# Gate and up projections by seven block products of 256 columns, the other engines' order from due times

## The chip, the cores and the metric

The kernel runs on one core of a Trainium2 chip. The metric is the time of one execution on the device in microseconds (us), the median of several runs. The core has a matmul engine (PE, with its weight loads shown apart as PEld) and three elementwise engines: DVE (VectorE), ACT (ScalarE) and POOL (GpSimd). SP is the queue that issues the weight transfers. PE writes to the accumulator memory PSUM, the other tiles lie in SBUF.

## The reference, cut to what matters

Two decoder layers on 512 tokens of width 1024 in float32. Each layer has a SwiGLU half step, a mixer and another SwiGLU half step: four half steps in all (`ffn` with j = 0 to 3). The change is to the half steps.

```python
D_MODEL, SEQ, D_FF = 1024, 512, 2816

def swiglu(x, wg, wu, wd):
    return (jax.nn.silu(x @ wg) * (x @ wu)) @ wd

h = x
for l in range(DEPTH):
    h = h + 0.5 * swiglu(rmsnorm(h, norm_ffn1[l]), ffn1_wg[l], ffn1_wu[l], ffn1_wd[l])
    hn = rmsnorm(h, norm_mix[l])
    ...
    h = h + mix.astype(h.dtype)
    h = h + 0.5 * swiglu(rmsnorm(h, norm_ffn2[l]), ffn2_wg[l], ffn2_wu[l], ffn2_wd[l])
return rmsnorm(h, final_norm)
```

## The kernel before

Activations are held transposed: 8 tiles `h[0]` to `h[7]` of 128 channels by 512 tokens. Every float32 operand of a matmul is split into a rounded part (hi) and the rest (lo), and `mm3` makes one product of blocks as three matmuls: hi by hi, lo by hi, hi by lo. Each matmul has 128x128 weights, loaded before it, and 512 moving columns, the tokens. In row names `pg<-xl,wh` the first input is the moving one, the second the weights.

A half step has 22 feature tiles of 128 features. For each, the gate tile `pg` and the up tile `pu` are made by `proj`: 8 channel blocks by `mm3`, 24 matmuls. DVE multiplies `pg` and `pu` by the row norm `rstd` (L316, L323), ACT takes Silu (L318), DVE multiplies the two (L325), ACT and DVE split the result into `ahi` and `alo` (L328, L329). The feature tiles come in parts of 8, 7 and 7; after each part eight down products `pd`, one per channel tile, add the part into `h[d]` (L372).

Weights are streamed once. `Stream` fetches units of 128x1024 floats (512 KB) into three raw buffers `wr`, ACT rounds each half into `wh` (L182), DVE subtracts to get `wl` (L186). In one stretch of the second mixer the subtraction is on POOL instead (L184).

At the start of a half step the sums of squares of `h` (`ssum`, L231 and L232) are turned into `rstd` by a short chain over PE, DVE, POOL, DVE, ACT, DVE, PE and ACT. For the very first half step DVE adds the squares between its first conversions; for the later ones POOL adds them at the end of the stage before.

The schedule is manual: every engine executes its instructions in the order in which the code issues them, and waits at the head of its own queue for semaphores. `W.pump()` after each tile decides where transfers and conversions are put: it converts two units ahead. No planner stands behind it.

## Time and profile before

| | us |
|---|---|
| median of 3 runs | 1925.91 (1925.67 to 1926.69) |
| the profiled execution, its own time | 1927.78 |
| its span, first to last instruction | 1926.0 |
| PE busy | 1906.6 |
| PEld busy | 1574.9 |
| DVE busy | 1015.7 |
| ACT busy | 723.0 |
| POOL busy | 206.4 |

The profiled execution is 1.87 us above the median, and 1.78 us of it lies outside the span. PE busy is a union of overlapping records: a 512-column matmul is recorded with 389 ns, while the next one starts sooner, so rates are read from starts and not from durations. Weight loads overlap the matmuls.

### The profile page before, as it was taken

How to read it: one execution, taken by the hardware profiler on the slowest of the kernel's cores; microseconds unless marked ns; L12 is line 12 of the kernel's file. 1: busy time of each engine (PE TensorE's matmuls, PEld its weight loads, DVE VectorE, ACT ScalarE, POOL GpSimd, SP SyncE). 2: the span in 40 equal slices, each digit the busy share in tenths (PEclk: the TensorE clock that was granted, in tenths of full speed). 3: DMA queues.
4: the chain of work that ended last, by engine and by line, in shares of the span. 5: the costliest groups of instructions: out<-in, count | busy, mean ns of one | idle time of the engine just before them, and what ended most of it. 6: DMA issues, size and time to landing. Idle time of an engine off the chain costs nothing.

```text
span 1926.0 us, 23329 instructions
## 1 busy us (share of the span) xinstructions
PE 1906.6 (99%) x8972; PEld 1574.9 (82%) x8972; DVE 1015.7 (53%) x1734; ACT 723.0 (38%) x1475; POOL 206.4 (11%) x267
## 2 busy tenths in 40 slices
PE   8999999999999999999999999999999999999998
PEld 6888888778888888888888888878887788888886
DVE  6534444656654344446444434566888654344443
ACT  5322222443432232224322323336888543222223
POOL 0000000203100000002000000113556410000001
PEclk9999999999999999999999999999999999999999
DMA  4323232221232222323322232242000233232322
GB/s 163 105 88 109 79 112 87 87 94 65 78 110 98 96 100 79 110 81 105 105 91 99 92 105 96 80 139 74 29 29 26 65 100 99 88 108 80 111 89 73
DMA packets 52751, 174.62 MB, mean 91 GB/s; under 512 B 6496, under 2 KB 8720, under 8 KB 52640
## 3 DMA queue, kind: packets, MB, share of 16 engines
q1 hardware_dynamic: 51328, 171.67, 26.9%
q8 instruction: 71, 1.16, 0.3%
q10 hardware_dynamic: 576, 1.05, 0.1%
q0 software_dynamic: 736, 0.41, 0.1%
q14 instruction: 40, 0.33, 0.1%
HBM read 171.01 MB, written 2.10 MB: 90 GB/s over the span
## 4 chain that ended last, share of the span: by engine, by line
PE 96%; DVE 1%; ACT 1%; DMA 1%; issue 1%; POOL 0%; SPq 0%; POOLq 0%; ACTq 0%
PE pg L292 8%; PE pg L291 8%; PE pu L291 8%; PE pg L293 8%; PE pu L293 8%; PE pu L292 8%; PE pd L292 8%; PE pd L293 8%; PE pd L291 8%; PE pj L291 3%; PE pj L293 2%; PE pj L292 2%; PE X L762 2%; PE S L997 2%; PE T L1044 2%; PE O L1078 1%
## 5 line engine op out<-in xcount | busy, mean ns | idle before, releaser
L186 DVE TENSOR_TENSOR wl<-wr,wh 128x512 fp32r<-128x512 f32 (+1 forms) x622 | 415.3, 710 | 150.0 <-ACT wh L182 150.0
L182 ACT ACTIVATE wh<-wr 128x512 fp32r<-128x512 f32 (+3 forms) x640 | 357.6, 605 | 262.7 <-PE pd L292 190.7
L291 PE MATMUL pg<-xh,wh 128*128 128x512 f32 x704 | 275.7, 392 | 5.8 <-ACT wh L182 5.2
L292 PE MATMUL pg<-xl,wh 128*128 128x512 f32 x704 | 275.4, 391 | 0.6 <-DVE xl L223 0.6
L293 PE MATMUL pg<-xh,wl 128*128 128x512 f32 x704 | 275.1, 391 | 0.0
L291 PE MATMUL pu<-xh,wh 128*128 128x512 f32 x704 | 274.3, 390 | 0.0
L293 PE MATMUL pu<-xh,wl 128*128 128x512 f32 x704 | 273.9, 389 | 0.0
L292 PE MATMUL pu<-xl,wh 128*128 128x512 f32 x704 | 273.9, 389 | 0.0
L291 PE MATMUL pd<-ahi,wh 128*128 128x512 f32 x704 | 273.9, 389 | 0.0
L292 PE MATMUL pd<-alo,wh 128*128 128x512 f32 x704 | 273.9, 389 | 0.0
L293 PE MATMUL pd<-ahi,wl 128*128 128x512 f32 x704 | 273.9, 389 | 0.0
L232 POOL TENSOR_TENSOR ssum<-ssum,sq 128x512 f32<-128x512 f32 x41 | 53.2, 1297 | 1456.3 <-issue 978.9
L328 ACT ACTIVATE ahi<-av 128x512 fp32r<-128x512 f32 x88 | 55.7, 633 | 377.4 <-DVE av L325 377.4
L372 DVE SCALAR_TENSOR_TENSOR h<-pd,h 128x512 f32<-128x512 f32 (+1 forms) x97 | 66.4, 686 | 228.3 <-PE pd L293 228.3
L291 PEld LDWEIGHTS pg<-xh,wh 128*128 128x128 f32 x704 | 132.9, 189 | 34.4 <-ACT wh L182 5.2
L292 PEld LDWEIGHTS pg<-xl,wh 128*128 128x128 f32 x704 | 132.9, 189 | 29.3 <-DVE xl L223 1.7
L323 DVE TENSOR_TENSOR t<-pu,rstd 128x512 f32<-128x512 f32 x88 | 60.8, 691 | 181.2 <-PE pu L293 181.2
L318 ACT ACTIVATE sg<-t 128x512 f32<-128x512 f32 x88 | 55.6, 632 | 266.8 <-DVE t L316 266.8
L293 PEld LDWEIGHTS pg<-xh,wl 128*128 128x128 f32 x704 | 132.8, 189 | 27.4
L291 PEld LDWEIGHTS pd<-ahi,wh 128*128 128x128 f32 x704 | 132.2, 188 | 27.5
L293 PEld LDWEIGHTS pu<-xh,wl 128*128 128x128 f32 x704 | 132.2, 188 | 27.5
L292 PEld LDWEIGHTS pd<-alo,wh 128*128 128x128 f32 x704 | 132.2, 188 | 27.4
(340 smaller groups left out, 2581.4 us busy)
## 6 DMA issues: line engine op xcount, KB each, us to landing
wr<-in_wts_dram SPq DMA_DIRECT2D x259, 512.0 KB, 3.5
wr<-in_wts_dram SPq DMA_DIRECT2D x64, 448.0 KB, 3.2
h<-in_xt_dram SPq DMA_DIRECT2D x8, 256.0 KB, 5.0
cb<-in_cbias_dram SPq DMA_DIRECT2D x8, 128.0 KB, 3.5
out_dram<-ot ACTq DMA_DIRECT2D x4, 256.0 KB, 4.5
wr<-in_wts_dram SPq DMA_DIRECT2D x2, 456.0 KB, 5.4
out_dram<-ot SPq DMA_DIRECT2D x3, 256.0 KB, 5.0
wr<-in_wts_dram SPq DMA_DIRECT2D x4, 128.0 KB, 4.8
```

The source lines that it names most:

```text
L182: S.activation(hi[:, c], self.raw[j][:, c], AF.Copy)
L186: V.tensor_sub(lo[:, c], self.raw[j][:, c], f32(hi[:, c]))
L232: eng.tensor_tensor(self.ssum, self.ssum, sq, op=OP.add)
L291: TE.matmul(out, wh, xh, start=first, stop=False)
L292: TE.matmul(out, wh, xl, start=False, stop=False)
L293: TE.matmul(out, wl, xh, start=False, stop=last)
L318: S.activation(sg, t1, AF.Silu)
L323: V.tensor_mul(t2, pu, nm.rstd)
L328: S.activation(ahi, av, AF.Copy)
L372: V.scalar_tensor_tensor(h[d][:, c], pd[:, c], 0.5, h[d][:, c], op0=OP.mult, op1=OP.add)
L762: TE.matmul(p, (hi, hi, lo)[i][:, c], (nm.xh, nm.xl, nm.xh)[i][k], start=n == 0, stop=n == 3 * KB - 1)
L997: TE.matmul(bk[:, c0:c0 + n], w[:, j * 128:(j + 1) * 128], keys[:, 0:n], start=start and j != 1, stop=stop, skip_group_check=True)
```

## The change

In each half step the first four feature tiles (two pairs, `PLAIN = 2`) are made as before. From the third pair on, the gate tiles of a pair (m even) and its up tiles (m odd) are made together, as a 2x2 block product in Winograd's form: the weights of two feature tiles are four blocks (two feature tiles by two channel halves of four blocks each), the activations four blocks (two channel halves by two token halves of 256), and seven products (numbered 1 to 7 in the code) take the place of eight. Each product is 4 blocks by `mm3` on 256 columns, 12 matmuls. There are 9 pairs, so 18 values of m, in each of the four half steps.

For this there are new operands. Sums of the activation blocks (`x_sums`, `x_dif`) are made once per half step, on DVE and ACT. Sums of the weight blocks (`T1` to `T4`) are made on POOL, four 128x512 operations per m. Five of the seven products use an operand that must then be split by ACT and DVE (`sh`, `sl`): T1 to T4 and the plain block B22. The other two use the blocks of the first raw unit, split as before. Partial results in PSUM are copied by ACT into `U` and combined by DVE between products, since later products accumulate on them.

The parts are 4, 4, 4, 4 and 6 tiles, and the down products of a part are put between the products of later m: `half_step` gives PE's order. From m = 5 to m = 20 one step of PE is 7 products and two down products of 12 matmuls (512 columns). A raw unit goes to one of three rings: `wr` (3 buffers), `wf` (1) and `wg` (2).

PE's order and SP's order of transfers are fixed by the code. The order on DVE, ACT and POOL is worked out at build: each step has a due time, counted back from PE's, and a list schedule with assumed costs picks the ready step that is due first; a POOL step and a DVE step marked `lock` are not put at the same time. The sorted order is then issued, so on the chip the order of every engine is fixed, as before. The order of the mixers is not changed.

```diff
 KB = D // 128
-PARTS = (8, 7, 7)
+PARTS = (4, 4, 4, 4, 6)
+PLAIN = 2
...
+def half_step():
...
+    ev = [(t, 2 * q + e) for q in range(PLAIN) for t in "gu" for e in range(2)]
+    m0, end = 2 * PLAIN, len(PARTS) - 1
+    d = [("d", p, i, 0, PARTS[p]) for p in range(end) for i in DORD]
+    for m in range(m0, 22):
+        x, y = (d.pop(0) if d and m > m0 else None for _ in range(2))
+        if m == m0:
+            ev += [(n, m) for n in (1, 2, 5, 6)]
+        else:
+            ev += [e for e in ((1, m), (2, m), (7, m - 1), (5, m), x, (6, m), (3, m - 1), (4, m - 1), y) if e]
+    ev += [(7, 21), (4, 21), (3, 21)] + [("d", end, i, 0, 4) for i in DORD[:2]]
+    return ev + [("d", end, i, 4 * (n < 2), PARTS[end]) for n, i in enumerate(DORD)]
+
...
+    class Step:
...
+        def add(self, eng, cost, fn, deps=(), bufs=(), lock=False):
...
+                for i in range(1, len(u)):
+                    f = u[i].touch[0]
+                    f.deps += [x for x in [u[i - 1].touch[0]] + (u[i - r.n].touch if i >= r.n else []) if x is not f]
...
+            at = 0
+            for s in steps:
+                if s.eng == "PE":
+                    s.due = at
+                    at += s.cost
...
+                if s.due is None:
+                    s.due = min([n.due - self.HOP for n in s.next] + [at]) - s.cost
...
+            free = {"PE": 0, "SP": 0, "DVE": 2000, "ACT": 1500, "POOL": 1500}
...
+                            continue
+                        other = held["POOL"] if e == "DVE" else held["DVE"] if e == "POOL" else 0
+                        begin = lambda s: max(free[e], ready[s], other if s.lock or e == "POOL" else 0)
+                        first_ = min(begin(s) for s in can[e])
+                        s = min((s for s in can[e] if max(free[e], ready[s]) <= first_ + 30), key=lambda s: (s.due, s.n))
+                        k = (begin(s), s.due)
...
+                (t, _), s, e = best
+                (can if e in can else line)[e].remove(s)
+                end = t + s.cost
+                free[e] = t + 1900 if e == "SP" else end
+                if s.lock or e == "POOL":
+                    held[e] = end
...
+            return [s for t, s in sorted(out, key=lambda x: (x[0], x[1].n))]
...
+        def run(self):
+            for s in self.order():
+                s.fn()
...
+            def x_sums(k):
+                g0, g1 = nm.gain(k), nm.gain(k + 4)
+                q, t, s = Buf(Rq), Buf(RU), Buf(Rx)
+                s1 = act(256, lambda: S.activation(q.t[:, A], h[k + 4][:, B], AF.Copy, scale=g1), (), (q,))
+                s1 = dve(325, lambda: V.scalar_tensor_tensor(t.t[:, A], h[k][:, B], g0, q.t[:, A], op0=OP.mult, op1=OP.add),
+                         (s1,), (q, t), True)
+                s2 = dve(325, lambda: V.scalar_tensor_tensor(t.t[:, B], h[k][:, A], g0, t.t[:, A], op0=OP.mult,
+                                                             op1=OP.subtract), (s1,), (t,), True)
+                s3 = dve(325, lambda: V.scalar_tensor_tensor(q.t[:, B], h[k + 4][:, A], g1, t.t[:, B], op0=OP.mult,
+                                                             op1=OP.add), (s2,), (q, t), True)
...
+                xsum[k] = (s, s2, s3)
+
+            def x_dif(k, dep):
...
+                s = dve(256, lambda: V.tensor_sub(q.t[:, A], h[k][:, A], h[k][:, B]), (), (q,), True)
+                s = act(256, lambda: S.activation(nm.xh[k][:, B], q.t[:, A], AF.Copy, scale=g), (s, dep), (q,))
+                xdif.append(dve(325, lambda: V.scalar_tensor_tensor(
+                    nm.xl[k][:, B], q.t[:, A], g, f32(nm.xh[k][:, B]), op0=OP.mult, op1=OP.subtract), (s,), (q,), True))
...
+                s1 = gps(sub(t["T1"], lambda: b1.t[:, H0], lambda: b0.t[:, H0]), (l0, l1), (t["T1"], b0, b1))
+                s2 = gps(sub(t["T2"], lambda: t["T1"].t, lambda: b1.t[:, H1]), (s1, l1), (t["T2"], t["T1"], b1))
+                s4 = gps(sub(t["T4"], lambda: b0.t[:, H1], lambda: t["T2"].t, OP.add), (s2, l0), (t["T4"], t["T2"], b0))
+                s3 = gps(sub(t["T3"], lambda: b1.t[:, H1], lambda: b1.t[:, H0]), (l1,), (t["T3"], b1))
...
+            def operand(n, m):
+
...
+                w = Buf(Rs)
+                s = act(T, lambda: S.activation(w.t[0], src(), AF.Copy), (dep,), (w, b))
+                return w, dve(T, lambda: V.tensor_sub(w.t[1], src(), f32(w.t[0])), (s,), (w, b), True)
...
+            def product(n, m):
+                u = m % 2
+                if n == 1:
+                    u0, u1 = load("wf" if u else "wr"), load("wg")
+                    convert(u0)
+                    pair[m] = {"w": con[u0], "r1": raw[u1], "t": sums(m, raw[u0], raw[u1]), "xy": Buf(Rxy)}
...
+                dep += {5: [x[1] for x in xsum.values()], 3: [x[2] for x in xsum.values()], 7: xdif}.get(n, [])
+                dep += [p[x] for x in {6: ("e2", "e2c"), 7: ("e6",), 4: ("e7",), 3: ("e7c",)}.get(n, ())]
+                acc = z if n in (5, 3) else xy
...
+                def mm():
+                    o, q, r = {1: (0, A, 0), 2: (4, A, 0), 7: (0, B, 0), 4: (4, B, 0), 5: (0, slice(0, 256), 1),
+                               6: (0, slice(256, 512), 1), 3: (0, slice(512, 768), 1)}[n]
+                    out, (hi, lo) = acc.t[:, B if n == 2 else A], ws()
...
+                        start = k == 0 and n in (1, 5)
+                        TE.matmul(out, wh, xh[:, q], start=start, stop=False, skip_group_check=True)
+                        TE.matmul(out, wh, xl[:, q], start=False, stop=False, skip_group_check=True)
+                        TE.matmul(out, wl, xh[:, q], start=False, stop=k == 3, skip_group_check=True)
+
+                done = p[n] = pe(1440, mm, dep, (w, acc))
...
+                if n == 2:
+                    U = p["U"] = Buf(RU)
+                    p["c"] = c0, c1 = [Buf(Rcu if u else Rcg) for _ in range(2)]
+                    p["e2"] = act(256, lambda: S.activation(U.t[:, B], xy.t[:, A], AF.Copy), (done,), (xy, U))
+                    p["e2c"] = dve(256, lambda: V.tensor_add(c0.t[:, A], xy.t[:, B], U.t[:, B]), (p["e2"],), (xy, U, c0))
+                    return
+                if n in (1, 5):
...
+                if n == 6:
+                    p["e6"] = act(256, lambda: S.activation(U.t[:, A], xy.t[:, A], AF.Copy), (done,), (xy, U))
+                elif n == 7:
+                    p["e7"] = act(256, lambda: S.activation(U.t[:, B], xy.t[:, A], AF.Copy), (done, p["e2c"]), (xy, U))
+                    p["e7c"] = dve(256, lambda: V.tensor_add(c1.t[:, B], z.t[:, A], U.t[:, B]), (p["e7"], p[5]), (z, U, c1))
+                elif n == 3:
+                    p["e3"] = dve(256, lambda: V.tensor_add(c1.t[:, A], z.t[:, A], U.t[:, A]), (done, p["e6"]), (z, U, c1))
+                if 3 in p and 4 in p:
+                    x1 = dve(256, lambda: V.tensor_mul(c0.t[:, A], c0.t[:, A], nm.rstd[:, A]), (p["e2c"], rstd), (c0,), True)
+                    y = dve(T, lambda: V.tensor_mul(c1.t, c1.t, nm.rstd), (p["e3"], p["e7c"], rstd), (c1,), True)
+                    x2 = dve(256, lambda: V.tensor_mul(c0.t[:, B], xy.t[:, A], nm.rstd[:, B]), (p[4], rstd), (xy, c0))
+                    if not u:
+                        sg[m] = [(c0, act(T, lambda: S.activation(c0.t, c0.t, AF.Silu), (x1, x2), (c0,))),
+                                 (c1, act(T, lambda: S.activation(c1.t, c1.t, AF.Silu), (y,), (c1,)))]
...
+                        s = sg.pop(m - 1)
+                        finish(m // 2, 0, c0, (x1, x2), s[0])
+                        finish(m // 2, 1, c1, (y,), s[1])
...
+            def down(p, d, k0, k1):
+                f0, n = sum(PARTS[:p]), PARTS[p]
+                if k0 == 0:
+                    u = load("wr")
+                    convert(u)
+                    pds[d] = (Buf(Rpd), con[u])
...
+                s = pe(681 * (k1 - k0), mm, [*ends] + [ah[f0 + k][1] for k in range(k0, k1)],
+                       [w, b] + [ah[f0 + k][0] for k in range(k0, k1)])
```

Two places in the program's order on DVE, of before and of the change.

The first is DVE at the start of the first half step, from the conversion of the second weight unit on (`wl`), with the sums of squares (`ssum`). Before:

```order
L186 TENSOR_TENSOR wl<-wr,wh 128x512 x2
L232 TENSOR_TENSOR ssum<-ssum,sq 128x512 x3
L186 TENSOR_TENSOR wl<-wr,wh 128x512 x4
L232 TENSOR_TENSOR ssum<-ssum,sq 128x512 x4
L266 TENSOR_SCALAR var<-pn 128x4
L277 TENSOR_SCALAR sq<-ident,rc 128x128 x4
L279 TENSOR_TENSOR dgl<-sq,dgh 128x512
```

After the change the same place on DVE reads as follows; `U`, `xs` and `sq` of 128x256 are the block sums of `x_sums`:

```order
L218 TENSOR_TENSOR wl<-wr,wh 128x512 x2
L271 TENSOR_TENSOR ssum<-ssum,sq 128x512 x3
L796 TENSOR_TENSOR ssum<-ssum,sq 128x512 x4
L628 SCALAR_TENSOR_TENSOR U<-h_72,vec,sq 128x256
L630 SCALAR_TENSOR_TENSOR U<-h_72,vec,U 128x256
L632 SCALAR_TENSOR_TENSOR sq<-h_76,vec,U 128x256
L628 SCALAR_TENSOR_TENSOR U<-h_73,vec,sq 128x256
L630 SCALAR_TENSOR_TENSOR U<-h_73,vec,U 128x256
L637 TENSOR_TENSOR xs<-sq,xs 128x256
L632 SCALAR_TENSOR_TENSOR sq<-h_77,vec,U 128x256
L636 TENSOR_TENSOR xs<-U,xs 128x512 x2
L541 TENSOR_TENSOR wl<-wr,wh 128x512 x6
```

The conversion of the third and fourth unit (`wl` x4 before, the first of `wl` x6 now) stood after three sums of squares; it now stands behind all seven and behind the block sums of two channel blocks. ACT's order has the same shift: its conversion of the third unit stands behind its squares and the copies for those block sums.

The second place is DVE inside the first half step, between matmul tiles, with buffer numbers in the names. Before, for one feature tile and the start of the next:

```order
L329 TENSOR_TENSOR alo_373<-av_370,ahi_372 128x512
L186 TENSOR_TENSOR wl_402<-wr_249,wh_401 128x512 x2
L316 TENSOR_TENSOR t1_409<-pg_376,rstd_336 128x512
L186 TENSOR_TENSOR wl_439<-wr_312,wh_438 128x512 x2
L323 TENSOR_TENSOR t2_446<-pu_413,rstd_336 128x512
L325 TENSOR_TENSOR av_448<-sg_411,t2_446 128x512
L329 TENSOR_TENSOR alo_451<-av_448,ahi_450 128x512
```

After the change, from the first combination of an m (L721) on, in the steady stretch; `sl` are the split operands of T1 to T4, `cg` and `cu` the combined gate and up tiles:

```order
L721 TENSOR_TENSOR cg_1648<-xy_1593,U_1643 128x256
L541 TENSOR_TENSOR wl_1646<-wf_1548,wh_1645 128x512 x2
L730 TENSOR_TENSOR cu_1673<-z_1469,U_1457 128x256
L677 TENSOR_TENSOR sl_1670<-T4_1403,sh_1669 128x512
L677 TENSOR_TENSOR sl_1691<-T3_1589,sh_1690 128x512
L769 SCALAR_TENSOR_TENSOR h1_73<-pd_1677,h1_73 128x512
L541 TENSOR_TENSOR wl_1713<-wr_1611,wh_1712 128x512
L677 TENSOR_TENSOR sl_1732<-T1_1641,sh_1731 128x512
L732 TENSOR_TENSOR cu_1673<-z_1469,U_1457 128x256
L677 TENSOR_TENSOR sl_1748<-T2_1675,sh_1747 128x512
L736 TENSOR_TENSOR cu_1465<-xy_1407,rstd_400 128x256
L606 TENSOR_TENSOR cu_1465<-cu_1465,cg_1279 128x512
```

For the work of one m DVE had eight 128x512 operations. It now has ten of 128x512 and five of 128x256, on average over gate and up, and among them stand the conversion (`wl`) and the addition into `h` of two down products, one 128x512 operation each.

## Rows read from the trace of the kernel before

**Rows 1.** The page: busy us (share of the span) per engine, granted clock in 40 slices.

```profile
PE 1906.6 (99%) x8972; PEld 1574.9 (82%) x8972; DVE 1015.7 (53%) x1734; ACT 723.0 (38%) x1475; POOL 206.4 (11%) x267
...
PEclk9999999999999999999999999999999999999999
```

**Rows 2.** The page: the chain that ended last, shares by engine.

```profile
PE 96%; DVE 1%; ACT 1%; DMA 1%; issue 1%; POOL 0%; SPq 0%; POOLq 0%; ACTq 0%
```

**Rows 3.** Windows: third half step: length, busy us of PE, PEld, DVE, ACT, POOL.

```profile
902.00:1262.00 360.00, 360.00 (x1593) 298.22 (x1592) 172.70 (x263) 110.95 (x199) 11.95 (x13) 1.00 0.29 97
```

**Rows 4.** Timeline, PE at 400 us (start, us): 512 columns, twelve matmuls apart.

```profile
400.22 0.39 PE L293 MATMUL po<-wh,xl 128*128 128x512 f32 x1
...
402.94 0.39 PE L293 MATMUL po<-wh,xl 128*128 128x512 f32 x1
```

**Rows 5.** Timeline, PE at 1305 us: 304 columns, 58 matmuls apart.

```profile
1305.53 0.30 PE L292 MATMUL pj<-wl,xh 128*128 128x304 f32 x1
...
1313.62 0.30 PE L293 MATMUL pj<-wh,xl 128*128 128x304 f32 x1
```

**Rows 6.** Timeline, PE at 1318 us: two matmuls of 256 columns and the next.

```profile
1318.61 0.40 PE L997 MATMUL S<-kA,qA 128*128 128x256 f32 x2
1318.85 0.28 PE L1005 MATMUL S<-negb,identb 128*128 128x256 bf16 x1
```

**Rows 7.** Groups by line and form: busy us, mean ns: the loads of those 256-column matmuls.

```profile
L997 PEld LDWEIGHTS S<-kA,qA 128*128 128x128 f32 x128 | 23.1, 190 | 2.7 <-ACT P L1023 0.9
```

**Rows 8.** Groups by line and form, DVE, ACT and POOL: busy us, mean ns.

```profile
L186 DVE TENSOR_TENSOR wl<-wr,wh 128x512 fp32r<-128x512 f32 x551 | 382.5, 732 | 150.0 <-ACT wh L182 150.0
L182 ACT ACTIVATE wh<-wr 128x512 fp32r<-128x512 f32 x569 | 328.5, 619 | 262.7 <-PE pd L292 190.7 <-issue 46.8 <-DMA wr<-in_wts_dram 15.2
...
L316 DVE TENSOR_TENSOR t<-pg,rstd 128x512 f32<-128x512 f32 x88 | 60.8, 691 | 122.1 <-PE pg L293 119.8 <-ACT rstd L287 2.2
...
L232 POOL TENSOR_TENSOR ssum<-ssum,sq 128x512 f32<-128x512 f32 x41 | 53.2, 1297 | 1456.3 <-issue 978.9 <-ACT sq L231 477.5
...
L223 DVE SCALAR_TENSOR_TENSOR xl<-h,vec,xh 128x512 fp32r<-128x512 f32 x48 | 37.9, 798 | 37.3 <-ACT xh L222 37.1
...
L612 DVE SCALAR_TENSOR_TENSOR S<-S,dc,at 128x128 f32<-128x128 f32 x12 | 4.2, 348 | 0.4
...
L1093 DVE TENSOR_TENSOR ce<-S,cb 128x256 f32<-128x256 f32 x8 | 3.4, 423 | 1.1 <-PE S L1088 0.9
...
L1099 ACT ACTIVATE ce<-ce 128x256 f32<-128x256 f32 x8 | 3.3, 407 | 1.0 <-DVE ce L1098 1.0
```

**Rows 9.** Timeline, DVE and POOL at 349 us, and DVE at 400 us without POOL.

```profile
349.23 1.29 POOL L232 TENSOR_TENSOR ssum<-ssum,sq 128x512 f32<-128x512 f32 x1 [3.49 <-ACT sq L231]
...
349.64 1.90 DVE L186 TENSOR_TENSOR wl<-wr,wh 128x512 fp32r<-128x512 f32 x2 [0.29 <-ACT wh L182]
...
400.77 1.28 DVE L186 TENSOR_TENSOR wl<-wr,wh 128x512 fp32r<-128x512 f32 x2
```

**Rows 10.** Timeline, POOL and DVE at 1348 us, where DVE reads PSUM.

```profile
1348.16 2.52 POOL L184 TENSOR_TENSOR wl<-wr,wh 128x512 fp32r<-128x512 f32 x2
1348.53 0.68 DVE L769 SCALAR_TENSOR_TENSOR qf<-X,rstd 128x512 f32<-128x512 f32 x1
```

**Rows 11.** Timeline, start of the first half step: DVE and PE.

```profile
14.03 1.30 DVE L186 TENSOR_TENSOR wl<-wr,wh 128x512 fp32r<-128x512 f32 x2 [0.43 <-ACT wh L182]
...
15.36 0.39 PE L291 MATMUL pu<-xh,wh 128*128 128x512 f32 x1
...
15.59 2.29 DVE L232 TENSOR_TENSOR ssum<-ssum,sq 128x512 f32<-128x512 f32 x3 [0.27 <-ACT sq L231]
...
20.20 3.08 DVE L232 TENSOR_TENSOR ssum<-ssum,sq 128x512 f32<-128x512 f32 x4
...
20.80 0.39 PE L291 MATMUL pg<-xh,wh 128*128 128x512 f32 x1
```

**Rows 12.** The page: weight transfers, count, KB each, us from issue to landing.

```profile
wr<-in_wts_dram SPq DMA_DIRECT2D x259, 512.0 KB, 3.5
```

More of the change, by code (lines that the diff above doesn't have):

```diff
@@ L275, in rms_diag @@
         dg = npl.tile([128, T], F32, name="sq", bufs=2)
[L276 to L277 removed]
+        rms_blocks(dg, rc)
         S.activation(hi, dg, AF.Copy)
@@ new lines, in ffn @@
+            fs = c.enter_context(pool(f"fs{j}", 1, reuse_waits="tile"))
+            ps = c.enter_context(pool(f"fp{j}", 3, space=PSUM, reuse_waits="tile"))
+            pl = Plan()
+            A, B = slice(0, 256), slice(256, T)
+            H0, H1 = slice(0, T), slice(T, 2 * T)
+            pe = lambda cost, fn, deps=(), bufs=(): pl.add("PE", cost, fn, deps, bufs)
+            act = lambda n, fn, deps=(), bufs=(): pl.add("ACT", 100 + n, fn, deps, bufs)
+            dve = lambda n, fn, deps=(), bufs=(), lock=False: pl.add("DVE", 155 + n, fn, deps, bufs, lock)
@@ new lines, in ffn, with hi @@
+            end = at
+            for u in range(end, min(end + NRAW, len(sel))):
+                load("wr")
+            for u in range(end, min(end + 2, len(sel))):
+                w = Buf(Rh)
+                for c0 in (0, T):
+                    if c0 < units[sel[u]][1]:
+                        b, ld = raw[u]
+                        def hi(u=u, c0=c0, w=w):
+                            W.hi[u], W.lo[u] = w.t
+                            W.half_hi(u, c0)
+                        s = act(T, hi, (ld,), (b, w))
+                        dve(T, lambda u=u, c0=c0: W.half_lo(u, c0), (s,), (b, w), True)
@@ L380, in mixer0 @@
+            pl.run()
+            for d in (W.raw, W.hi, W.lo):
+                for u in [u for u in d if u < end]:
+                    del d[u]
+            W.i, W.nd, W.ncv = end, at, min(end + 2, len(sel))
     def mixer0(nm, nxt):
```

447 lines of the change are left out of this document (342 added, 105 removed).

## The prediction, on record before the change was run

> **What bounds the kernel now.** I began with the page. PE is busy for 99% of the span and its clock is granted at the full 2.4 GHz in every slice [rows 1]. The chain of waits says the same from the other side: 96% of it is PE [rows 2]. Then the windows by stage: the third half step is PE from end to end, 360.00 of 360.00 us, while DVE works 172.70 [rows 3]; the other three read alike (369, 361 and 351 us of PE). So a half step costs what its matmuls cost, and DVE and ACT have half their time free.
>
> The duration of a matmul record is not its price, because records overlap. I read starts: twelve matmuls of 512 columns lie between two rows 2.72 us apart, 226.7 ns each [rows 4]. A half step has 44 tiles of 24 and 22x24 for the down products, 1584 matmuls; four of them are 1437 us, about three quarters of the span, which agrees with the windows.
>
> **The change, part by part.** *Fewer columns on PE.* For one m, two tiles of 24 matmuls (48x226.7 ns = 10.88 us) become seven products of 12, 84 matmuls of 256 columns. If time went with columns alone this would be 7/8. What decides is the fixed part of each matmul. 304 columns cost 8.09 us for 58, 139.5 ns [rows 5]. From 512 to 304 columns this is 0.419 ns a column, so 256 columns come to 139.5 - 48x0.419 = 119.4 ns. Two 256-column matmuls in the second mixer start 0.24 us before the next one, 120 ns [rows 6]. I take 119.5; the starts are given to 0.01 us, so two matmuls in [rows 6] leave bounds of about 117 and 122. An m then costs 84x119.5 ns = 10.04 us and saves 0.84; 18 m in four half steps save 72x0.844 = **61 us** (76 at 117 ns, 46 at 122).
>
> The Trainium skill has its own figure for this ("TensorE: Matmul & The Clock Gate", section Back-to-back issue gap): 262 cycles for 256 columns, 109 ns, and 518 for 512, 216 ns. Every row here is some 11 ns above it (226.7 for 512), so the rows decide; at 109 ns the saving would be 123 us, an estimate from that page.
>
> *More weight loads.* Each matmul loads its weights. A half step goes from 1584 to 8x24+18x84+22x24 = 2232 loads, 2592 more in all. Loads are recorded with 190 ns [rows 7], longer than the 120 ns between starts of the very matmuls they feed [rows 6], so they overlap each other and I cost them at nothing. If that cover were gone, a 256-column matmul would cost 190 ns.
>
> *More work on DVE, ACT and POOL.* I take a step of PE as the unit: seven products and two down products, 10.04 + 24x0.2267 = 15.48 us. Before, the same work took 10.88 + 5.44 = 16.32. In a step DVE has on average 14 operations of 128x512 (two conversions of the first raw unit, five operand splits, the norm product, two of the four that finish the up tiles, two conversions and two additions for the down products) and 5 of 128x256. At 691 and 423 ns [rows 8] this is 9.67 + 2.12 = 11.8 us; L186's mean of 732 holds some blocked ones. ACT has 11 of 128x512 and three of 128x256, at 619 and 407 ns [rows 8] some 8.0 us. POOL has four, 4x1297 ns = 5.2 us [rows 8]. Each alone fits under 15.48.
>
> DVE and POOL don't simply add up, nor are they independent. Where POOL adds two SBUF tiles, DVE's two `wl` beside it took 1.90 us; elsewhere two in a row take 1.28 [rows 9]. So 0.62 was lost after a head start of 0.41 for POOL; at worst, both starting together, 1.03 per POOL operation. Where DVE reads PSUM, the same kind of POOL operation costs it nothing: 0.68 us under 2.52 of POOL [rows 10]. In a step six of the 19 DVE operations read PSUM, 3.1 us that can lie under POOL's 5.2. So DVE needs from 11.8 up to 11.8 + 4x1.03 = 15.9 us. I take 14, as part of POOL lies under the PSUM operations and back-to-back operations are shorter, 0.64 each [rows 9]. That is 1.5 us under PE's step. DVE is also ahead: with four split operands and three converted units in the rings, order and code put a split 7 to 12 us before its product.
>
> The Trainium skill states this as a rule ("SBUF — State Buffer", section Who interferes with whom): DVE with two SBUF inputs and a POOL operation that reads SBUF block each other fully. The trace agrees in kind, with 0.62 us here; full blocking without any overlap is a rival below.
>
> *The start of the first half step.* Before, DVE converted units three and four between the third and fourth sum of squares. Now the order puts all seven sums and the block sums of two channel blocks ahead. In the trace DVE ends the second unit at 15.3, needs 2.29 us for three sums and 3.08 for four, and PE begins its third tile at 20.80 [rows 11]. So the sums end near 21.0. Then come five dependent operations of 128x256, at about 0.52 us (an estimate between the 348 ns of 128 and the 798 of 512 columns [rows 8], with a hop between engines), to 23.5, ACT's copy behind them (0.6), and only then its conversion (0.62): 24.8. The low half follows on DVE a little later. PE waits some 4 to 5.5 us: I take **5.2**. The bounds are 0 (the sums fit in the slack) and 8. The other half steps begin with about ten microseconds of converted tiles and without those sums, so the block sums hide there.
>
> *The rest.* The order of transfers changes, not their amount; a 512 KB unit lands in 3.5 us [rows 12] and is asked for most of a step ahead. Combinations between products (ACT's copy, DVE's addition, 0.407 + 0.423 us) have 5.6 us of other products and a down product before they are needed. At the end of a half step the last up tile's chain (addition, norm, product, rounding, rest: 0.42 + 0.69 + 0.69 + 0.62 + 0.69 = 3.1 us) has two partial down products of 2.72 in front. I cost these at nothing, and all unlisted waits of PE together at 2 us, half a microsecond per half step, with 0 and 8 as bounds.
>
> *Sum.* 1927.8 (the profiled execution) - 61 + 5.2 + 2 = 1874. The median of the runs is 1.9 below that execution, so **1872 us**.
>
> **The rivals.** *DVE and POOL set the pace a little:* at 15.9 us a step, 0.42 over PE in 64 steps, 27 us come back: 1899. For it speaks that DVE goes from half busy to at least three quarters; against it the PSUM operations.
>
> *DVE and POOL fully in turn* (the side of slower): nothing of POOL under DVE's operations, 11.8 + 5.2 = 17.0 us a step. It decides from 16.3 on, the step before. 64x1.5 = 97 us come back: 1969. Against it stands the unhindered operation in [rows 10]; for it, that most of DVE's operations read two SBUF tiles and the order is fixed at build with costs that the chip may not keep.
>
> *Loads bind:* 256-column matmuls at 190 ns give 16.0 us an m, 5.1 more than before, 72 times: about 2290. The Trainium skill points this way ("Perfetto Trace Analysis", section Identifying the Most-Contended Engine): it judges PE's headroom by the busy share of its loads, and 2592 more records of 190 ns make over 2000 us, longer than the span. Against it speaks that matmuls 120 ns apart are fed by loads of 190 [rows 6, 7].
>
> *No fixed part in long runs of short matmuls:* 256x0.419 = 107 ns, 9.0 us an m, 135 us saved instead of 61, about 1798. Against it stands the run of 58 with 139.5 where 304x0.419 would be 127 [rows 5]. The 109 ns of the Trainium skill's page ("TensorE: Matmul & The Clock Gate", named above) lie near this case, and no run here shows them yet.
>
> *A queue waits for something late in every step* (a PSUM buffer, a raw buffer), 0.8 us each: the gain is gone, 1925. The order gives no such place, but it shows no times.
>
> **How the numbers follow.** The forecast (PE sets the pace, 1860 to 1887 with the bounds of 256 columns and of the start) has 0.62; DVE and POOL a little, 0.18; fully in turn, 0.10; loads, 0.03; no fixed part, 0.03; the late queue, 0.04. The range reaches from 1858 to 1912 and so takes in the first two, 0.80. A measurement of this kernel tells about 0.2% (4 us) from no change. Faster: 0.62 + 0.18 + 0.03 = 0.83. Same: 0.04. Slower: 0.13.
>
> **What would show it.** Right: starts of 256-column matmuls about 119.5 ns apart in long rows; half steps of some 344 us each, PE still over 98% busy, the first one about 5 us longer; DVE near 14 us busy per 15.5. Wrong: idle time of PE before products that ends with DVE's `sl` or ACT's `sh` (pace by DVE and POOL), DVE operations near 1.4 us throughout, or starts of 140 ns and more (loads).

## The result, and the profile after

The changed kernel takes **1883.38 us** (median of four runs, 1881.94 to 1884.09), the kernel before 1926.11 beside it (1925.67 to 1926.69). The ratio is 0.9777, with a 95% interval from 0.976 to 0.9794: faster by 2.2%. The forecast was 1872, 11 us too low; the time lies inside the range of 1858 to 1912. The profiled execution took 1881.94 us, its span is 1880.1. Two executions, one of 4691.39 us with one more POOL operation and one of 2209.98 us without due times, are far slower than the other three of their kernels and are left out of the medians below.

The page of the changed kernel: busy us, share of the span and instructions of each engine, and the granted clock.

```profile
PE 1853.3 (99%) x11564; PEld 1651.5 (88%) x11564; DVE 1474.6 (78%) x2414; ACT 969.7 (52%) x1971; POOL 636.3 (34%) x555
...
PEclk9999999999999999999999999999999999999999
```

Against [rows 1], PE has 2592 more matmuls and is still busy for 99% of a span that is 46 us shorter. DVE went from 53% to 78%, POOL from 11% to 34%. The windows show the third half step, 348.00 us where [rows 3] had 360.00, with 286 us of DVE in it in place of 173, and a row for 300 us of its middle (columns as in [rows 3]; the last three are the granted clock, the share of DMA and its GB/s).

```profile
876.30:1224.30 348.00, 346.64 (x2241) 317.33 (x2240) 286.09 (x432) 171.10 (x322) 116.87 (x80) 1.00 0.29 100
...
900.00:1200.00 300.00, 298.64 (x2025) 277.51 (x2024) 249.53 (x375) 145.47 (x275) 106.44 (x72) 1.00 0.28 98
```

The timeline of PE around 708 us shows what a matmul costs now (start, us).

```profile
706.47 0.28 PE L711 MATMUL xy<-xh,sh 128*128 128x256 f32 x1
...
709.35 0.40 PE L342 MATMUL pd<-ahi,wh 128*128 128x512 f32 x1
709.59 0.40 PE L343 MATMUL pd<-alo,wh 128*128 128x512 f32 x1
709.82 0.39 PE L344 MATMUL pd<-ahi,wl 128*128 128x512 f32 x1
710.05 0.40 PE L342 MATMUL pd<-ahi,wh 128*128 128x512 f32 x1
710.28 0.39 PE L343 MATMUL pd<-alo,wh 128*128 128x512 f32 x1
710.51 0.39 PE L344 MATMUL pd<-ahi,wl 128*128 128x512 f32 x1
...
712.10 0.28 PE L711 MATMUL xy<-xs,sh 128*128 128x256 f32 x1
```

Between the first two rows lie 24 matmuls of 256 columns in 2.88 us, 120.0 ns each; the forecast had 119.5 from [rows 5, 6]. Then come twelve of 512 columns, in 2.75 us and not in the 2.72 of [rows 4]: the first five take 1.16 us, 232 ns each, the other seven 227. Over all rows of the trace the medians of these five are 233, 236, 228, 233 and 231 ns, and behind a down product the second start of 256 columns comes 114 ns after the first: a change to 512 columns and back costs 21 ns, at 132 places 2.8 us. The prediction had no term for it.

The weight loads that feed the short matmuls, grouped by line and form (busy us, mean ns):

```profile
L711 PEld LDWEIGHTS z<-xs,sh 128*128 128x128 f32 x576 | 110.6, 192 | 0.0
```

They are recorded with 192 ns, as in [rows 7], while the matmuls start 120 ns apart: more loads cost nothing. The list of PE's waits (total us, times, longest) names the rest, here with the two longest of the kernel before ahead of it.

```profile
PE pg L291 <- ACT wh L182: 5.2, 1, 5.2
PE T L1044 <- DVE PTl L1064: 2.6, 6, 0.8
...
PE xy L342 <- ACT wh L206: 5.0, 1, 5.0
PE xy L342 <- ACT wh L538: 4.6, 1, 4.6
PE T L1514 <- DVE PTl L1534: 2.6, 6, 0.8
PE xy L711 <- ACT U L729: 2.2, 4, 0.6
...
PE xy L711 <- DVE cg L721: 0.8, 1, 0.8
```

Of the changed kernel's list the first and the third stand in the kernel before as well. New are 4.6 us at L538, the third weight unit of the first half step, 4 x 0.6 at L729, and 0.8 once. The timeline shows the first of them with DVE and ACT:

```profile
17.78 3.08 DVE L796 TENSOR_TENSOR ssum<-ssum,sq 128x512 f32<-128x512 f32 x4
...
19.47 0.39 PE L344 MATMUL z<-xh,wl 128*128 128x512 f32 x1
...
23.79 2.17 ACT L538 ACTIVATE wh<-wr 128x512 fp32r<-128x512 f32 x4
...
24.46 0.60 PE L342 MATMUL xy<-xh,wh 128*128 128x512 f32 x1 [4.60 <-ACT wh L538]
```

In [rows 11] the third tile begins at 20.80; here it begins at 24.46, behind all sums of squares and block sums, as the prediction laid out (24.8). Then something follows that it did not have, in the windows of that stretch:

```profile
18.00:24.40 6.40, 1.86 (x9) 1.20 (x7) 5.98 (x12) 4.71 (x10) 0.00 (x0) 1.00 0.01 5
24.40:28.20 3.80, 3.41 (x8) 2.21 (x9) 3.80 (x8) 2.91 (x7) 0.00 (x0) 0.55 0.23 43
28.20:36.00 7.80, 7.80 (x40) 6.52 (x39) 3.15 (x9) 1.52 (x3) 1.42 (x1) 1.00 0.59 202
```

Behind the gap the clock is granted at 0.55 on average, most of the stretch at the lower level of 1.2 GHz, and matmuls of 512 columns start 427 ns apart in place of 227. The eight starts that follow the one at 19.47 reach to 28.11, 8.64 us in place of 8 x 0.227: the gap, the slow matmuls and a wait of 0.33 us among them together cost 6.8 us.

The wait at L729 stands at the end of each half step:

```profile
326.81 0.28 PE L713 MATMUL xy<-xh,sl 128*128 128x256 f32 x1
327.23 0.36 ACT L729 ACTIVATE U<-xy 128x256 f32<-128x256 f32 x1
327.62 0.42 DVE L730 TENSOR_TENSOR cu<-z,U 128x256 f32<-128x256 f32 x1 [1.15 <-ACT U L729]
327.64 0.39 PE L711 MATMUL xy<-xh,sh 128*128 128x256 f32 x1 [0.56 <-ACT U L729]
```

Product 7 of the last m ends, ACT copies its result out, and only then may product 4 accumulate on the same bank; in the last m nothing stands between the two. The starts are 0.83 us apart, 0.71 more than 120 ns, in four half steps 2.8 us.

Last, DVE and POOL in the middle of a half step: groups by line and form (the third one adds down products, read from PSUM, into `h`), and one collision in the timeline.

```profile
L541 DVE TENSOR_TENSOR wl<-wr,wh 128x512 fp32r<-128x512 f32 x280 | 264.2, 962 | 6.7 <-ACT wh L538 3.2 <-PE pd L571 1.3
L677 DVE TENSOR_TENSOR sl<-T,sh 128x512 fp32r<-128x512 f32 x288 | 245.4, 861 | 25.0 <-ACT sh L676 22.4
L769 DVE SCALAR_TENSOR_TENSOR h<-pd,h 128x512 f32<-128x512 f32 x159 | 109.1, 686 | 55.6 <-PE pd L344 54.7
```

```profile
707.45 1.29 POOL L657 TENSOR_TENSOR T<-wg,wr 128x512 f32<-128x512 f32 x1 [9.52 <-DMA wg<-in_wts_dram]
707.61 3.40 DVE L541 TENSOR_TENSOR wl<-wr,wh 128x512 fp32r<-128x512 f32 x2
708.83 1.63 POOL L657 TENSOR_TENSOR T<-T,wg 128x512 f32<-128x512 f32 x1
```

Two conversions that take 1.28 us alone [rows 9] take 3.40 beside two POOL operations. PE does not notice: its row of starts above runs through the same microseconds without a gap. Over all records the same holds by kind: of the 288 splits at L677 those with more than 0.3 us of a POOL addition beside them take 1229 ns on average, those with none 682; the additions at L769, with one input from PSUM, take 683 beside POOL and 688 without.

### The profile page after: what moved, and what is told of

It is laid out like the page before. It is cut to its first block, busy times and chain, and to the rows that moved or that the text cites. A ratio compares the mean times of both kernels' runs of the same rounds, so it can differ in the third digit from the quotient of the medians.

```text
span 1880.1 us, 30824 instructions
## 1 busy us (share of the span) xinstructions
PE 1853.3 (99%) x11564; PEld 1651.5 (88%) x11564; DVE 1474.6 (78%) x2414; ACT 969.7 (52%) x1971; POOL 636.3 (34%) x555
## 5 line engine op out<-in xcount | busy, mean ns | idle before, releaser
L538 ACT ACTIVATE wh<-wr 128x512 fp32r<-128x512 f32 (+1 forms) x312 | 179.3, 603 | 202.6 <-PE pd L343 172.8
L677 DVE TENSOR_TENSOR sl<-T,sh 128x512 fp32r<-128x512 f32 x288 | 245.4, 861 | 25.0 <-ACT sh L676 22.4
L676 ACT ACTIVATE sh<-T 128x512 fp32r<-128x512 f32 x288 | 180.5, 627 | 57.9 <-PE z L713 55.0
L711 PE MATMUL xy<-xh,sh 128*128 128x256 f32 x576 | 163.4, 284 | 2.2 <-ACT U L729 2.2
L712 PE MATMUL z<-xs,sh 128*128 128x256 f32 x576 | 163.0, 283 | 0.0
L711 PE MATMUL z<-xs,sh 128*128 128x256 f32 x576 | 163.0, 283 | 0.0
L713 PE MATMUL xy<-xh,wl 128*128 128x256 f32 x576 | 163.0, 283 | 0.0
L713 PE MATMUL z<-xs,sl 128*128 128x256 f32 x576 | 163.0, 283 | 0.0
L712 PE MATMUL xy<-xl,sh 128*128 128x256 f32 x576 | 163.0, 283 | 0.0
L712 PE MATMUL xy<-xl,wh 128*128 128x256 f32 x576 | 163.0, 283 | 0.0
L713 PE MATMUL xy<-xh,sl 128*128 128x256 f32 x576 | 163.0, 283 | 0.0
L769 DVE SCALAR_TENSOR_TENSOR h<-pd,h 128x512 f32<-128x512 f32 (+1 forms) x161 | 109.8, 683 | 59.0 <-PE pd L344 58.1
```

The source lines that it names most:

```text
L538: S.activation(w.t[0][:, c], b.t[:, c], AF.Copy)
L676: s = act(T, lambda: S.activation(w.t[0], src(), AF.Copy), (dep,), (w, b))
L677: return w, dve(T, lambda: V.tensor_sub(w.t[1], src(), f32(w.t[0])), (s,), (w, b), True)
L711: TE.matmul(out, wh, xh[:, q], start=start, stop=False, skip_group_check=True)
L712: TE.matmul(out, wh, xl[:, q], start=False, stop=False, skip_group_check=True)
L713: TE.matmul(out, wl, xh[:, q], start=False, stop=k == 3, skip_group_check=True)
```

## The experiments

The theory at this point: PE sets the pace; the products save 72 x (10.88 - 84 x 0.120) = 58 us, and some 13 us go back at named places (start, tails and one more wait, changes of column count). The rivals: DVE and POOL are at their limit and take part of the gain; the fixed part of a matmul is something else, such as the load; or the new order, not the products, made the gain. Times are compared by medians, each with the kernel before on the same chip (1926.0 to 1926.5).

**The start.**

```diff
-                    f.deps += [x for x in [u[i - 1].touch[0]] + (u[i - r.n].touch if i >= r.n else []) if x is not f]
+                    f.deps += [x for x in ([u[i - 1].touch[0]] if u[i - 1].tile_ is None else []) + (u[i - r.n].touch if i >= r.n else [])
+                               if x is not f]
```

> The planner no longer makes a buffer's first step wait for the first step of the buffer before it in the ring when that earlier buffer was already filled ahead of the half step. So the conversion of the third weight unit may start before PE touches the second one. Theory (a false wait in the order makes the stall at the start): DVE converts the third unit before the last four sums of squares, PE's gap of 4.8 us before its third tile and the stretch at the half clock behind it go, and the time falls by 6 to 7 us to about 1876. Rival (DVE simply has too much to do there, whatever the order): the gap moves behind the third or fourth tile, and at most 2 us are won, about 1882.

Measured: 1879.62 us (ratio 0.9759, 0.9745 to 0.9772), 3.8 below the changed kernel. In the trace of this kernel the conversion of the third unit stands ahead of the last four sums:

```profile
17.92 1.29 DVE L542 TENSOR_TENSOR wl<-wr,wh 128x512 fp32r<-128x512 f32 x2
19.12 3.08 DVE L797 TENSOR_TENSOR ssum<-ssum,sq 128x512 f32<-128x512 f32 x4
...
33.15 0.51 PE L571 MATMUL pd<-dgh,ones_r 128*128 128x512 f32 x1 [0.88 <-ACT dgh L561]
```

The gap before the third tile is gone, and the half clock behind it (1.00 granted from 24.40 to 28.20). So the false wait in the order made the stall. That is read from the trace: the intervals of the two ratios overlap, so the times alone would not show 3.8 us. But part came back: the row norm is later, and PE stands 1.5 us longer around its two matmuls at 33 us; and the first product 6 of each half step now waits for DVE's `cg`, four gaps of 0.45 to 0.94 us where the changed kernel had one of 0.96. The rival, that DVE has too much to do at the start in any order, holds for that part.

**The tail.**

```diff
+    ev[-1:] = [(7, 21), (4, 20), (4, 21), (3, 21)]
-    ev += [(7, 21), (4, 21), (3, 21)] + [("d", end, i, 0, 4) for i in DORD[:2]]
+    ev += [("d", end, i, 0, 4) for i in DORD[:2]]
```

> In the last lines of a half step product 4 of m = 20 is put between products 7 and 4 of m = 21; nothing else changes. Theory (PE waits 0.72 us for ACT's copy between these two products once in each half step, and it lies on the path): the four gaps go, 4 x 0.72 = 2.9 us, about 1880.5. Rival (PE would wait a little later for the same chain, before the first full down product of the last part): no change, 1883.

Measured: 1879.84 us (0.9757, 0.9744 to 0.977), 3.5 below the changed kernel. No wait at that line is left in the trace. The theory holds by the trace; the time, whose interval overlaps that of the changed kernel, has 0.6 us more than the four gaps, which is inside the spread of the runs.

**Halves:** the gate and up tiles of the kernel before in 256-column matmuls. In this kernel each of the two halves opens its accumulation in the bank on its own, which changes what is added up, not which matmuls run.

```diff
+    def mm3h(out, wh, wl, xh, xl, first, last):
+        for x, y, s, e in ((wh, xh, first, False), (wh, xl, False, False), (wl, xh, False, last)):
+            for c in (slice(0, 256), slice(256, T)):
+                TE.matmul(out[:, c], x, y[:, c], start=s, stop=e, skip_group_check=True)
```

> The kernel before, with each 512-column matmul of the gate and up tiles issued as two of 256 columns: 176 tiles with 48 matmuls in place of 24, the same columns, twice the weight loads. Theory (a fixed part of 13.3 ns per matmul, 120 against 226.7 / 2): 4224 more matmuls x 13.3 ns = 56 us, about 1982. Rival (no fixed part in long rows): 1926. Rival (loads of 190 ns bind where they are the only thing between short matmuls): 48 x 190 = 9.1 us a tile against 5.4, about 2570.

Measured: 1981.39 us (1.0285, 1.0271 to 1.0299). 4224 more matmuls cost 54.9 us, 13.0 ns each. By the prediction's 119.5 ns and [rows 4] it would be 2 x 119.5 - 226.7 = 12.3 ns; both rivals are out by more than 50 us.

**Mixed**: only channel blocks 1, 3 and 5 of each tile in halves.

```diff
-            mm3(out, hi[:, k * ncol:(k + 1) * ncol], lo[:, k * ncol:(k + 1) * ncol],
+            (mm(k) if mm else mm3)(out, hi[:, k * ncol:(k + 1) * ncol], lo[:, k * ncol:(k + 1) * ncol],
...
+mm=lambda k: mm3h if k in (1, 3, 5) else mm3
```

> The kernel before, with the matmuls of channel blocks 1, 3 and 5 of each gate and up tile issued as two of 256 columns, so that a tile changes three times from 256 to 512 columns. Theory (the first five 512-column matmuls behind a row of 256-column ones start 233, 236, 228, 233 and 231 ns apart in place of 227, whatever the matmuls belong to): the fixed part gives 176 x 9 x 13.3 ns = 21 us and the changes some 0.06 us a tile, 11 us, about 1958; the first three 512-column matmuls behind each change are 233, 236 and 228 apart. Rival (the longer starts belong to the down products, for instance to their operands): 227 apart everywhere, about 1947.

Measured: 1952.40 us, one run. The timeline of PE in this kernel (rows of 512 columns between rows of 256):

```profile
701.62 0.40 PE L291 MATMUL pg<-xh,wh 128*128 128x512 f32 x1
701.86 0.40 PE L292 MATMUL pg<-xl,wh 128*128 128x512 f32 x1
702.09 0.39 PE L293 MATMUL pg<-xh,wl 128*128 128x512 f32 x1
702.32 0.28 PE L298 MATMUL pg<-xh,wh 128*128 128x256 f32 x1
```

The first three matmuls behind a change take 0.70 us, not 0.68; over the 524 changes inside tiles their medians are 233, 236 and 228 ns. So the longer starts follow the change of column count and have nothing to do with the down products. The time lies between the two figures expected, since I left out what the short matmuls give back: the six behind a change back start 116 to 121 ns apart, 10 ns less than six times 120. With that the sum is 1926.5 + 21 + 11 - 5, about 1953.

**One more POOL operation for each m.**

```diff
+                s3 = gps(sub(t["T3"], lambda: b1.t[:, H1], lambda: b1.t[:, H0]), (s3,), (t["T3"], b1))
```

> The changed kernel with the sum T3 of weight blocks made twice for each m: five POOL operations of 128x512 in a step of PE in place of four. In the trace of the changed kernel DVE is busy 14.36 us of a step of 15.48 in the middle of a half step, 2.5 us above its own 11.8, so one POOL operation takes some 0.64 us from DVE. Theory (PE sets the pace, DVE has about 1.1 us left): DVE rises to about 15.0 a step, the time stays within 4 us of 1883. Rival (DVE and POOL work fully in turn and are at the limit already): one more POOL operation of 1.4 us in each of 64 steps is paid in full or nearly, 1930 to 1970.

Measured: 1888.89 us (0.9805, 0.9789 to 0.9822), 5.5 above the changed kernel, with intervals that just overlap. That is a little more than the 4 us of the theory and far from the 47 that the rival asks at least: with DVE and POOL in turn and no time left, 64 operations of 1.4 us would have cost about 90. So DVE is not at its limit. This kernel has no trace that can be read, so where the 5.5 us arise is not shown. (The 14.36 us of the expectation are one step; the mean over the 300 us above is 12.9.)

**Twice the POOL operations:** each of the four lines for T1, T2, T4 and T3 stands twice, as the one above.

> The changed kernel with all four sums of weight blocks (T1 to T4) made twice for each m: eight POOL operations in a step. Theory (0.64 us of DVE lost per POOL operation, PE's step of 15.48 is the floor): DVE needs 14.36 + 4 x 0.64 = 16.9 us a step, 1.4 over PE in 64 steps, some +90 us, about 1975. Rival (the loss per operation is bounded by what DVE does beside PSUM reads, and the order at build finds room): up to +20 us, under 1905. Rival (fully in turn): 11.8 + 8 x 1.4 = 23 us a step, +480 us, about 2360.

Measured: 2100.40 us (1.0905, 1.0888 to 1.0921), 217 above the changed kernel: 3.4 us in each of 64 steps, where I expected 1.4. The windows and PE's waits of this kernel:

```profile
700.00:900.00 200.00, 179.71 (x1158) 164.73 (x1157) 160.64 (x206) 72.90 (x145) 133.15 (x87) 0.92 0.25 88
```

```profile
PE pd L344 <- DVE wl L541: 46.1, 12, 3.9
PE xy L715 <- DVE cg L725: 38.0, 20, 2.3
PE xy L715 <- DVE cu L725: 35.3, 20, 3.4
```

The pace is off PE: it waits for conversions and combinations on DVE. But DVE is 80% busy here and POOL 67%, so neither is full; that the order fixed at build makes each wait for the other is likely, but not shown. And with PE's waits the granted clock falls, to 0.92 in this stretch. The distances of PE's starts divide the 217 us: held against 227 and 120 ns, and where the clock is at the lower level against the 427 and 213 ns seen there, some 159 us are waits and some 58 are matmuls at the lower level, an estimate from the two traces. How far collisions, and how far the order, make the waits was not separated. The rival of the prediction is real, then; it begins between one and four more POOL operations in a step.

**The sums on DVE.**

```diff
-                s1 = gps(sub(t["T1"], lambda: b1.t[:, H0], lambda: b0.t[:, H0]), (l0, l1), (t["T1"], b0, b1))
+                s1 = dve(T, sub(t["T1"], lambda: b1.t[:, H0], lambda: b0.t[:, H0]), (l0, l1), (t["T1"], b0, b1), True)
```

and the same for T2, T4 and T3, with DVE as the engine in `sub`.

> The changed kernel with the four sums T1 to T4 on DVE in place of POOL, so that POOL has almost nothing to do in a half step. Theory (DVE's own work is what counts, a sum costs it 0.69 us and a POOL operation costs it 0.64): DVE needs 11.8 + 4 x 0.69 = 14.6 us a step, still under 15.48, and the time stays within 5 us of 1883. Rival (a chain of three sums ahead of the splits on one engine makes PE wait): 0.7 us and more at the first products of each m, 72 x 0.7 = 50 us, about 1935.

Measured: 1882.02 us (0.9773, 0.9757 to 0.979), no different from the changed kernel. Its window and groups:

```profile
900.00:1200.00 300.00, 299.44 (x2031) 278.41 (x2030) 254.43 (x448) 146.56 (x277) 0.00 (x0) 1.00 0.28 99
```

```profile
L677 DVE TENSOR_TENSOR sl<-T,sh 128x512 fp32r<-128x512 f32 x288 | 198.0, 689 | 32.2 <-ACT sh L676 25.9
L541 DVE TENSOR_TENSOR wl<-wr,wh 128x512 fp32r<-128x512 f32 x280 | 187.6, 684 | 4.8 <-ACT wh L538 3.3 <-PE pd L571 1.3
```

With 73 more operations DVE is busy 254.4 us of 300, against 249.5 with the sums on POOL. Without those 73 at 0.688 it would be 204.2: on POOL the 72 sums of this stretch take 45.3 us from DVE, 0.63 each. A sum on POOL costs DVE nearly what it would cost on DVE itself.

**An order without regard to collisions.**

```diff
-            self.eng, self.cost, self.fn, self.lock = eng, cost, fn, lock
+            self.eng, self.cost, self.fn, self.lock = eng, cost, fn, False
...
-                        begin = lambda s: max(free[e], ready[s], other if s.lock or e == "POOL" else 0)
+                        begin = lambda s: max(free[e], ready[s], 0)
```

> The changed kernel with an order worked out as if DVE and POOL never held each other up (no step is marked, POOL's steps start when they are ready). Theory (DVE has slack, so where POOL's operations lie among DVE's does not matter much): within 8 us of 1883. Rival (the planned order is what keeps the collisions at 0.64 us per POOL operation): at 1.4 us each DVE needs 11.8 + 5.6 = 17.4 us a step, +120 us, about 2005; at 1.03 us 15.9 a step, about 1910.

Measured: 1899.39 us (0.9862, 0.9847 to 0.9876), 16 above the changed kernel, between the two. PE's waits and one of the places:

```profile
PE xy L711 <- DVE cg L721: 10.1, 4, 2.9
```

```profile
586.15 0.42 DVE L721 TENSOR_TENSOR cg<-xy,U 128x256 f32<-128x256 f32 x1
...
586.62 0.39 PE L711 MATMUL xy<-xs,sh 128*128 128x256 f32 x1 [2.87 <-DVE cg L721]
```

The cost is not spread over the steps, as both theories had it: it is one wait of 2.3 to 3.1 us in each half step, at its first product 6, where DVE still makes the block differences and the norm products of the plain tiles. Later in the half step DVE catches up: from 900 to 1200 us it is busy 253.3 us, against 249.5 with the marks, so the marks save it little. These four waits are ten of the 16 us. Most of the rest is the clock: behind three of the four it is granted at the lower level for a stretch, as here behind the first:

```profile
70.00:80.00 10.00, 10.00 (x68) 9.70 (x67) 7.23 (x13) 4.35 (x9) 2.11 (x2) 0.86 0.46 156
```

By the distances of the starts, matmuls at the lower level cost some 7 us in this trace and some 1 us in that of the changed kernel, an estimate.

**An order without due times.**

```diff
-key=lambda s: (s.due, s.n))
+key=lambda s: (ready[s], s.n))
```

> The changed kernel, where the list schedule at build picks among the ready steps of DVE, ACT or POOL the one that has been ready longest in place of the one that is due first. Theory (due times keep the operand of the next product ahead of work that can wait): with DVE busy 14.4 of 15.5 us a late operand isn't made up for; a PE wait of one DVE or ACT operation, 0.7 us, in most of the 64 steps and more at the starts, 45 us, about 1930. Rival (rings and tiles ready well ahead hide any sensible order): within 8 us of 1883.

Measured: 1891.24 us (0.9822, 0.9806 to 0.9838), 7.9 above the changed kernel, at the edge of the rival's 8. Again the waits stand at the beginning of the half steps (for `xh` L644 and `xl` L645, the block differences, together 6.1 us) and, but for the tails, none in the steps behind them.

**The order without the products.** All tiles plain, planner and parts as changed; `x_sums` and `x_dif` left out.

```diff
-    ev = [(t, 2 * q + e) for q in range(PLAIN) for t in "gu" for e in range(2)]
+    ev, f, end = [], 0, len(PARTS) - 1
+    for p, n in enumerate(PARTS):
+        t = [(x, y) for y in range(f, f + n) for x in "gu"]
+        f += n
+        ev += t[:1] + [("d", p - 1, i, 0, PARTS[p - 1]) for i in DORD if p] + t[1:]
```

> All 22 feature tiles of a half step made as before (two tiles of 24 matmuls of 512 columns, no product), with the new planner, the new parts of 4, 4, 4, 4 and 6 tiles and without the block sums. The matmuls are those of the kernel before. Theory (the products are the whole gain, the planner and the parts bring nothing): 1926, and a few us more for the start, up to 1932. Rival (a part of the 43 us comes from the order): below 1920; PE waits for so little in the kernel before that less than 1912 is not possible.

Measured: 1926.00 us (0.9999, 0.9989 to 1.0009). With plain tiles the planner and the finer parts bring and cost nothing; the products are the whole gain.

**The repairs together**, with the down products of a step side by side:

```diff
-(5, m), x, (6, m), (3, m - 1), (4, m - 1), y)
+(5, m), (6, m), (3, m - 1), (4, m - 1), x, y)
```

> Three edits on the changed kernel together: the start without the false wait, the tail of a half step with product 4 of m = 20 between products 7 and 4 of m = 21, and the two down products of a step next to each other, so that a step changes once from 256 to 512 columns. Theory (the parts are independent): 1883.4 - 3.8 (start alone) - 3.5 (tail alone) - 64 x 0.021 = 1.3 (half of the changes of column count; the first five 512-column matmuls behind a change lose 27 ns, the first 256-column one wins 6) = 1874.8. Rival (the start only moves DVE's work into the next stretch, and without a down product between products 5 and 6 the combinations come too late): PE waits 0.5 to 1 us in each of 64 steps, 1905 or more.

Measured: 1873.39 us (0.9728, 0.9714 to 0.9743), where the sum of the parts was 1874.8. The parts add up, and here the interval lies clear of the changed kernel's.

**The same with the sums on DVE:**

> The same three edits, and the sums T1 to T4 on DVE in place of POOL. Theory (a POOL operation takes from DVE what the sum itself would cost there, so the engine does not matter, and where DVE alone works its order comes out as planned): as the kernel with POOL, or better by the 2.5 us that PE still waits at the second m of the half steps, 1872 to 1875. Rival (DVE has more to do at the start of a half step, where it is the late one): 2 us more at each of four starts, 1883.

Measured: 1871.94 us (0.9719, 0.9705 to 0.9734). PE's waits in this kernel:

```profile
PE xy L343 <- ACT wh L207: 5.2, 1, 5.2
PE T L1516 <- DVE PTl L1536: 2.7, 7, 0.8
PE xy L343 <- ACT xh L257: 0.8, 1, 0.8
PE pd L572 <- ACT dgh L562: 0.7, 1, 0.7
```

No product waits any more. The 1.5 us to the kernel above are within the intervals; its two gaps at products (1.29 and 0.73 us) are gone here. Both beat the changed kernel, by 0.5% and 0.6%.

## Why the prediction was right, and where its 11 us went

The mechanism was right. The bound was PE, the gain came from fewer columns alone (all tiles plain: 1926.00), and DVE and POOL rose without taking the pace. Made against the profiled executions, as in the prediction, the sum reads so:

| term | forecast us | measured us |
|---|---|---|
| products, 72 m | -61 | -57.7 |
| start of the first half step | +5.2 | +6.8 |
| other waits of PE | +2 | +3.8 |
| changes of column count | none | +2.8 |
| half clock in the very first matmuls | none | -1.1 |
| sum | -54 | -45.4 |

The executions differ by 1927.78 - 1881.94 = 45.8 us. So the table covers 8 of the 11 us by which the forecast was too low. The other 3 lie in the last step of the sum, from the profiled execution to the median: the prediction took off 1.9 us, as in the kernel before, but the changed kernel's profiled execution is the fastest of its four and lies 1.4 us under their median. Its mean granted clock is 0.998, that of the other three 0.997; more of them is not recorded.

*Fewer columns.* The step was right and the size off by half a nanosecond: 120.0 in place of 119.5 ns, but 6048 times, 3.3 us (with the rounding of 10.04). The halves measured the fixed part directly, at 13.0 ns where the prediction's figures give 12.3. The Trainium skill's figure for this ("TensorE: Matmul & The Clock Gate", section Back-to-back issue gap), 109 ns, which the page gives for a matmul by itself, does not agree with these rows: the runs show 120. The sign "half steps of some 344 us" was missed for the same small terms: the third took 348.00, with 0.8 us for the half nanosecond, 0.7 for the changes of column count, 0.7 for its tail and 1.0 for one more wait.

*More weight loads.* Right: 192 ns recorded, 120 between starts, no wait.

*DVE, ACT and POOL.* Right in that PE keeps the pace: 249.5 us in 300 are 12.9 in a step of 15.5, where 14 was taken (bounds 11.8 and 15.9). DVE's own work was priced too high, 11.8 for the 10.5 that 204.2 us in 300 come to; the collisions add 2.3, where 14 left 2.2 for them. The price of a collision, 0.62 us from one row of [rows 9], came out at 0.63 over 72 operations; that one row gave the mean is luck, as a single split beside POOL takes up to 1.79 us, 1.1 more than alone. The rule of the Trainium skill ("SBUF — State Buffer", section Who interferes with whom), that the two block each other fully, would be seen as 1.3 to 1.6 us per POOL operation; the trace shows it at single places (2.1 us lost under 2.9 of POOL at 707 us) and not on average, as part of what lies under POOL's operations is work of DVE that reads PSUM, which they do not slow (683 and 688 ns, above).

*The start.* The chain was read right, and ended at 24.46 where 24.8 was forecast. The prediction took the order as given and did not ask what made it: a wait in the planner for a buffer that was long filled. Undoing it took away the gap. The matmuls at half the clock behind the gap, which are most of the 1.6 us between 5.2 and 6.8, were not in the sum.

*The rest.* Here the step failed that costs the end of a half step at nothing. The chain behind the last up tile does hide behind the partial down products, as argued; but inside the last m, product 4 stands right behind product 7, and the 5.6 us of other products and a down product that the prediction gives to each combination are not there. That costs four times 0.71 us; one wait of 0.96 us at a product 6 makes up the 3.8.

*Changes of column count.* In the half steps of before 512 columns follow 512, so the rows of the prediction could not show them; this term was missing.

The first matmuls of all run at the lower clock until about 11.0 us where it was 13.3 before, by the spacing of their starts (0.43 us), which the digit 9 of the first slice in [rows 1] hides. The 25th matmul starts 1.1 us earlier, 0.2 of them because the first one does. This belongs to no edit: in the kernel with all tiles plain the spacing changes at 12.0.

*The bounds.* Those of the terms do not give the 1860 to 1887 of the forecast: the price of 256 columns alone gives 1857 to 1887, and the start would widen that by 5.2 below and 2.8 above. The measured time lies inside either.

Of the rivals, DVE and POOL at the limit is the one that nearly holds: one more POOL operation in a step costs 5.5 us, four cost 217. Loads, no fixed part and the late queue are refuted by the halves and by PE's waits.

## What to carry to other kernels

When long matmuls are replaced by more and shorter ones, price them by the distance of starts at the new length, and add what stands only at the seams: the changes of length, the last piece of a loop where the usual work between two dependent products is missing, and the first piece where the helpers have the most to do. Where an order is worked out at build, look in it for waits that no data need; taking one out took away a gap of 4.6 us here, and 3.8 us of the time. Work given to POOL beside a DVE that reads two SBUF tiles is not free: measure it by moving it back.

## What the runs showed of the hardware

- Behind a row of 256-column matmuls the first five of 512 columns start 233, 236, 228, 233 and 231 ns apart and then 227, in the down products of the changed kernel and in the gate and up tiles of the mixed kernel alike; behind 512 columns the second start of 256 comes 114 to 116 ns after the first, where 120 is usual. What in the engine makes this is open.
- After 5 us with almost no PE work, some seven matmuls ran at the lower clock; in the order without regard to collisions it fell behind three of four gaps of 2.3 to 3.1 us (0.86 from 70 to 80 us) and stayed at 1.00 behind the one at 583 us (586.60 to 604.00), though that one took 3.03 us, so a short gap did not always bring it.
- 512 columns cost 227 ns and 2 x 256 cost 240, with a load per matmul in both.
- A DVE operation on two SBUF tiles takes 682 ns without a POOL addition beside it and 1229 on average with one; an operation of the same size with one input from PSUM takes 688 and 683.
